# Tiles at multiples of 2048 bytes, and seven pieces of side work moved, in a two-block transformer kernel

## The chip, the cores and the metric

The kernel runs on one core of a Trainium2 chip, as one program. The metric is the time of the whole program on the device, in microseconds (us); less is better. A core has a matrix engine (TensorE, PE in the rows; PEld is its weight load), a vector engine (VectorE, DVE), a scalar engine (ScalarE, ACT), GpSimd (POOL), and SyncE (SP), from which most transfers are issued. Each engine takes its instructions in the order of the program; semaphores hold an instruction back until what it reads is there.

## The reference

Two blocks of a transformer on 256 tokens of width 2048, in float32. The first block has four mixers side by side (sparse attention, a short convolution, a spatial gating unit and stick-breaking attention), an output projection and a gated FFN; the second has an attention layer and a retention layer, each followed by a layer norm.

```
def first_block(x, ...):
    h = rms_norm(x, norm_mix); proj = h @ w_in              # all four mixers' inputs
    o_a = nsa_attention(...); o_b = short_conv_mixer(b_cols, conv_w)
    o_c = spatial_gating_mixer(c_cols, sgu_w, sgu_b); o_d = stick_breaking_attention(...)
    mixed = rms_norm(stack([o_a, o_b, o_c, o_d]), group_gain)
    x = x + mixed @ w_out
    h = rms_norm(x, norm_ffn)
    return x + (silu(h @ w_ffn_gate) * (h @ w_ffn_up)) @ w_ffn_down

def spatial_gating_mixer(cols, sgu_w, sgu_b):
    u, v = split(gelu(cols), 2); v = layer_norm_noaffine(v)
    return u * (tril(sgu_w) applied to v + sgu_b)

def second_block(x, ...):
    x = layer_norm(ALPHA * x + attention_mixer(x, ...), ln_gain[0], ln_bias[0])
    x = layer_norm(ALPHA * x + retention_mixer(x, ...), ln_gain[1], ln_bias[1])
    return x
```

## The kernel before

All weights are streamed once from memory in units of 128 x 1024 values (wf). ScalarE rounds a unit to the F32R format (wh, L375), VectorE takes the rest, wf - wh (wl, L385), and TensorE multiplies with both, so that the product is nearly that of float32. Activations are kept in the same two parts, next to each other in one tile of 512 columns. job_T holds 128 x 128 of the weights and moves an activation tile: for each pair, 512 columns against wh (L452) and 256 against wl (L453). A unit is eight such pairs. job_N holds activations and moves weights (L475 to L477). The stages in the order of time are: the input projection with the four mixers (to about 326 us), the output projection wo (to 435), the FFN (to 1225), attention 2 (to about 1518), retention (to 2280), and the last layer norm and the output (to 2297.5).

Between the weight matmuls the rest of the computation is woven in as side tasks, Python generators. Each pair of matmuls counts 325 ns, and with every 650 ns of it each task's counter falls by one; yield n lets a task wait n such steps. At certain places a task is run to its end at once: S.drain, or when a job asks for an operand tile whose task is not done (XS). The order of the program on each engine is thus fixed when the kernel is built, by these steps.

```
def adv(self, ns):
    self.acc += ns
    while self.acc >= self.period:      # 650
        ...
            t[1] -= 1
            if t[1] <= 0 and t[2] and ...: self.step(t)
```

Side work that the change touches:

- the sparse attention, task A: scores softmax (sm), their transpose (L816), the product with vc (L821);
- the gating unit, task C: gelu of u (cu) and v (cv) by POOL, VectorE and ScalarE (gq), the norm of v (L1043), the product with sg (L1048, called pz in the code), its norm, its transposes (L725) and the scaled operand tiles xB[8] to xB[11] (L732 on ScalarE, L738 on VectorE);
- the convolution, task B: by_task filters slice i and ends with a product on POOL (L1077); ev_bb takes the gate's accumulator of slice i, adds its two halves (ev_sum: ScalarE copies one half, evt, L662; VectorE adds the other, evs, L664), multiplies into braw and accumulates the squares in bacc, on POOL for the slices 0 to 2 and on VectorE for slice 3; then come the column sums (pcs), the reciprocal root, a diagonal matrix bdg (L545), the product pb (L548) that spreads it, and the tiles xB[12] to xB[15];
- wo(0), the first of four output jobs, in eight chunks of one unit each; it reads xB in order, two tiles to a chunk, so chunk 4 starts with xB[8];
- in attention 2, og_task: the gating of head h (L1522) and the split of the result into the operand xA (L509, L511);
- LN.stat: the sums lns (POOL) and sums of squares lnq (L1372) of the first layer norm, and next to it gain, the operand xg of retention (L1648, L1651);
- the end: VectorE finds mean and scale of the 256 rows, nm is -mean times scale; TensorE transposes it (L1993), multiplies it with the gain rows gr and adds the bias (L2004, six products in float32 over two rows), and VectorE finishes six of the eight output tiles with it (L2011); SyncE and ScalarE send them.

## Time and profile before

| | us |
|---|---|
| median of 3 runs | 2287.87 (2285.02 to 2290.71) |
| the profiled execution | 2299.29 |
| its span, first to last instruction | 2297.5 |
| TensorE busy | 2271.2 |
| VectorE busy | 1534.2 |
| ScalarE busy | 1134.2 |
| POOL busy | 406.4 |
| moved by the transfers | 409.82 MB, 178 GB/s over the span |

The profiled execution is a single one, 11.4 us above the median of the unprofiled runs. Busy times are shares of its span; where an engine stands idle only counts if another one has nothing else to do at that moment. The end of the span lies 3.3 us behind VectorE's last operation.

### The profile page before, as it was taken

How to read it: one execution, taken by the hardware profiler on the slowest of the kernel's cores; microseconds unless marked ns; L12 is line 12 of the kernel's file. 1: busy time of each engine (PE TensorE's matmuls, PEld its weight loads, DVE VectorE, ACT ScalarE, POOL GpSimd, SP SyncE). 2: the span in 40 equal slices, each digit the busy share in tenths (PEclk: the TensorE clock that was granted, in tenths of full speed). 3: DMA queues.
4: the chain of work that ended last, by engine and by line, in shares of the span. 5: the costliest groups of instructions: out<-in, count | busy, mean ns of one | idle time of the engine just before them, and what ended most of it. 6: DMA issues, size and time to landing. Idle time of an engine off the chain costs nothing.

```text
span 2297.5 us, 32746 instructions
## 1 busy us (share of the span) xinstructions
PE 2271.2 (99%) x12423; PEld 1946.4 (85%) x12423; DVE 1534.2 (67%) x2368; ACT 1134.2 (49%) x1661; POOL 406.4 (18%) x384
## 2 busy tenths in 40 slices
PE   8999999999999999999999999999999999999998
PEld 7877888888888888888888888898888888888886
DVE  6666697755555565555558898888776676766554
ACT  5457545544443354444444556555444544445442
POOL 2224341111110011110002211742000000001120
PEclk9999999999999999999999999999999999999998
DMA  7643355565565555656565444555555555556553
GB/s 248 231 147 119 111 187 189 184 187 189 187 191 189 179 190 187 188 184 190 186 201 183 141 152 153 179 168 199 175 167 174 183 167 187 168 174 216 189 179 118
DMA packets 113757, 409.82 MB, mean 178 GB/s; under 512 B 12816, under 2 KB 13072, under 8 KB 113342
## 3 DMA queue, kind: packets, MB, share of 16 engines
q1 hardware_dynamic: 111456, 399.75, 54.1%
q0 software_dynamic: 1424, 6.86, 0.9%
q8 instruction: 97, 1.59, 0.3%
q10 hardware_dynamic: 720, 1.13, 0.1%
q14 instruction: 60, 0.49, 0.1%
HBM read 405.57 MB, written 4.21 MB: 178 GB/s over the span
## 4 chain that ended last, share of the span: by engine, by line
PE 87%; DVE 5%; ACT 1%; issue 1%; POOL 1%; POOLq 0%; DVEq 0%; ACTq 0%
PE st L452 39%; PE st L453 20%; PE st L475 7%; PE st L477 7%; PE st L476 7%; DVE wl L385 2%; PE mO L1889 1%; PE mA L855 1%; PE mS L1862 0%; PE st L443 0%; PE st L441 0%; PE st L442 0%; PE st L2004 0%; PE mO L836 0%; PE mT L1907 0%
## 5 line engine op out<-in xcount | busy, mean ns | idle before, releaser
L375 ACT ACTIVATE wh<-wf 128x1024 fp32r<-128x1024 f32 (+1 forms) x750 | 789.7, 1055 | 731.7 <-PE st L452 381.1
L385 DVE TENSOR_TENSOR wl<-wf,wh 128x1024 fp32r<-128x1024 f32 (+1 forms) x750 | 954.8, 1282 | 287.8 <-ACT wh L375 287.1
L452 PE MATMUL st<-xA,wh 128*128 128x512 f32 x2016 | 722.6, 402 | 8.1 <-DVE xA L515 6.8
L453 PE MATMUL st<-xA,wl 128*128 128x256 f32 x2016 | 567.8, 282 | 1.7 <-DVE wl L385 1.5
L452 PE MATMUL st<-xB,wh 128*128 128x512 f32 x1440 | 511.4, 399 | 2.4 <-DVE evs L664 1.8
L452 PEld LDWEIGHTS st<-xA,wh 128*128 128x128 f32 x2016 | 380.9, 189 | 100.9 <-DVE xA L515 6.7
L453 PE MATMUL st<-xB,wl 128*128 128x256 f32 x1440 | 404.3, 281 | 0.0
L453 PEld LDWEIGHTS st<-xA,wl 128*128 128x128 f32 x2016 | 382.6, 190 | 2.9 <-DVE wl L385 2.5
L452 PEld LDWEIGHTS st<-xB,wh 128*128 128x128 f32 x1440 | 271.3, 188 | 67.0 <-DVE evs L664 2.5
L453 PEld LDWEIGHTS st<-xB,wl 128*128 128x128 f32 x1440 | 272.4, 189 | 1.0
L452 PE MATMUL st<-act,wh 128*128 128x512 f32 x704 | 248.8, 399 | 0.0
L453 PE MATMUL st<-act,wl 128*128 128x256 f32 x704 | 197.9, 281 | 0.0
L475 PE MATMUL st<-wh,xB 128*128 128x512 f32 x448 | 175.5, 392 | 0.0
L476 PE MATMUL st<-wl,xB 128*128 128x512 f32 x448 | 174.7, 390 | 0.0
L477 PE MATMUL st<-wh,xB 128*128 128x512 f32 x448 | 174.6, 390 | 0.0
L452 PEld LDWEIGHTS st<-act,wh 128*128 128x128 f32 x704 | 132.4, 188 | 32.9
L664 DVE TENSOR_TENSOR evs<-st,evt 128x256 f32<-128x256 f32 x110 | 46.2, 423 | 145.6 <-ACT evt L662 145.4
L453 PEld LDWEIGHTS st<-act,wl 128*128 128x128 f32 x704 | 133.0, 189 | 0.0
L475 PE MATMUL st<-wh,xA 128*128 128x512 f32 (+2 forms) x320 | 122.6, 383 | 0.0
L476 PE MATMUL st<-wl,xA 128*128 128x512 f32 (+2 forms) x320 | 118.3, 370 | 0.9 <-DVE wl L385 0.9
L477 PE MATMUL st<-wh,xA 128*128 128x512 f32 (+2 forms) x320 | 118.4, 370 | 0.0
L1211 POOL TENSOR_TENSOR evs<-evs,R 128x256 f32<-128x256 f32 x44 | 32.4, 735 | 484.5 <-DVE evs L664 484.5
(447 smaller groups left out, 2611.7 us busy)
## 6 DMA issues: line engine op xcount, KB each, us to landing
wf<-in_w_c SPq DMA_DIRECT2D x264, 512.0 KB, 4.2
wf<-in_w_e SPq DMA_DIRECT2D x256, 512.0 KB, 3.8
wf<-in_w_d SPq DMA_DIRECT2D x112, 512.0 KB, 3.5
wf<-in_w_a SPq DMA_DIRECT2D x84, 512.0 KB, 3.6
wf<-in_w_b SPq DMA_DIRECT2D x32, 512.0 KB, 4.3
xr<-in_xT SPq DMA_DIRECT2D x16, 256.0 KB, 5.4
wf<-in_w_a SPq DMA_DIRECT2D x5, 420.0 KB, 3.8
dr<-d POOLq DMA_DIRECT2D x1, 2048.0 KB, 10.1
```

The source lines that it names most:

```text
L375: ACT.activation(wh[q][:, :n], wf[q][:, :n], AF.Copy)
L385: V.tensor_tensor(wl[q][:, :n], wf[q][:, :n], wh[q][:, :n].bitcast(F32), OP.subtract)
L452: PE.matmul(ps[m], hv[:, cs], x, start=kk == 0, stop=False)
L453: PE.matmul(ps[m][:, :T], lv[:, cs], x[:, :T], start=False, stop=kk == K - 1)
L475: PE.matmul(p, xh, h[:, o:o + n], start=kk == 0, stop=False)
L476: PE.matmul(p, xh, l[:, o:o + n], start=False, stop=False)
L477: PE.matmul(p, xl, h[:, o:o + n], start=False, stop=kk == K - 1)
L664: V.tensor_tensor(s, p[:, :T], t, OP.add)
L855: PE.matmul(pv[:, y, :], qT[i // 2][64 * g:64 * g + 64, i % 2, tt * P:tt * P + P], kT[64 * g:64 * g + 64, b, 0:W], start=True, stop=True)
L1211: G.tensor_tensor(s, s, R2, OP.mult)
L1889: PE.matmul(po, l[:, st_, o], r_[:, st_], start=i == 0, stop=i == 5)
```

## The change

Eight edits. The tile deps and the tile gq8, each of one column, become the two columns of one tile, so that every tile laid out behind them, from wf on, begins 32 bytes lower: the weight and operand tiles go from 32 bytes past a multiple of 2048 to that multiple. In task A two waits go from 1 to 3 and from 1 to 2 steps. In task C the wait ahead of pz goes from 1 to 5. ev_bb(2), the last convolution gate, copies the whole accumulator with ScalarE (evc) and adds the halves on POOL. wo(0) takes its last two chunks tile by tile. og_task of the heads 13 to 15 waits 1 step, not 10. The squares of the first layer norm's tiles 12 to 15 are added on POOL. At the end, gain and bias rows are prepared as five rows in F32R (gain in parts for the three rows of nm in parts, bias in two), so that the six products run in F32R; nm is made of both halves by one operation and split by two more.

```diff
-    deps = pc.tile([P, 1], F32, name="deps")
+    two = pc.tile([P, 2], F32, name="two")
+    deps, gq8 = two[:, 0:1], two[:, 1:2]
...
             V.tensor_tensor(w, w, cmk[:, None, 15 * tt:15 * tt + nk].to_broadcast([P, 8, nk]), OP.mult)
-            yield 1
+            yield 3
             pt = mA()
             PE.transpose(pt[:120, :P], sc, ident)
             pcT = small(128)
             V.tensor_copy(pcT[:120], pt[:120, :P])
-            yield 1
+            yield 2
...
-    gq8 = pc.tile([P, 1], F32, name="gq8")
...
             u = yield from gelu2(cu[tt], 512, s2)
-            yield 1
+            yield 5
             pz = mA()
...
     def ev_bb(i0):
         def f(m, p):
             i = i0 + m
-            s = ev_sum(p)
+            if i0:
+                c = s2("evc")
+                ACT.activation(c, p, AF.Copy)
+                s = c[:, :T]
+                G.tensor_tensor(s, s, c[:, T:], OP.add)
+            else:
+                s = ev_sum(p)
             S.drain(tBy[i])
...
-    job_T(take(), xB, ev_wo(0))
+    job_T(take(), xB, ev_wo(0), 2)
...
-                (G if k < 12 else V).tensor_tensor(self.q, self.q, sq, OP.add)
+                (G if k < 12 or self.done else V).tensor_tensor(self.q, self.q, sq, OP.add)
...
-        yield 10
+        yield 10 if h < 13 else 1
         yield from split(x, s)
...
-    gr = q5.tile([P, D], F32, name="gr")
-    G.dma_start(gr[:2], a["lnv"])
...
+    gr = q5.tile([P, 3 * 512], F32R, name="gr")
+    def gr_task():
+        yield 8
+        for m in range(3):
...
+            for z, (lo, hi) in enumerate(((0, 3), (3, 5))):
+                G.dma_start(t[lo:hi], bass.AP(tensor=v.tensor, offset=v.offset + z * D + 512 * m,
+                                              ap=[[0, hi - lo], [1, 512]]))
+            yield 12
+            o = gr[:5, 512 * m:512 * m + 512]
+            ACT.activation(h, t, AF.Copy)
+            V.tensor_tensor(t, t, h.bitcast(F32), OP.subtract)
+            V.tensor_scalar(t, t, pick[:5, 1:2], None, OP.mult)
+            V.scalar_tensor_tensor(o, h.bitcast(F32), pick[:5, 0:1], t, OP.mult, OP.add)
+            yield 4
...
-    for tt in range(2):
-        V.scalar_tensor_tensor(nm[tt][:, 0:1], mv[:, 2 * tt:2 * tt + 1], -1.0, r[:, tt:tt + 1], OP.mult, OP.mult)
+    V.scalar_tensor_tensor(nm, mv[:, 0::2], -1.0, r, OP.mult, OP.mult)
+    V.tensor_copy(nx[:, :, 0:2], nm[:, :, None].to_broadcast([P, 2, 2]))
+    V.tensor_tensor(nx[:, :, 2], nm, nx[:, :, 0].bitcast(F32), OP.subtract)
...
-        PE.matmul(p, nT[tt][:2, :], gr[:2, 512 * m:512 * m + 512], start=True, stop=True)
+        PE.matmul(p, nT[tt][:5, :], gr[:5, 512 * m:512 * m + 512], start=True, stop=True)
```

How this changes the order on the engines, at three places. First POOL at the end of the convolution: L1077 is the filter's last product of slice 3, evs and evc are the gate's sum for a slice, braw, bq and bacc are slice 2. Before:

```order
L706 TENSOR_TENSOR gq<-gq,cu 128x512
L1077 TENSOR_TENSOR evs<-evs,R_121 128x256
L1095 TENSOR_TENSOR braw<-evs 128x256
L1100 TENSOR_TENSOR bq<-braw 128x256
L1101 TENSOR_TENSOR bacc<-bacc,bq 128x256
```

and now, with line numbers of the changed kernel:

```order
L708 TENSOR_TENSOR gq<-gq,cu 128x512
L1078 TENSOR_TENSOR evs<-evs,R_121 128x256
L1095 TENSOR_TENSOR evc<-evc 128x256
L1102 TENSOR_TENSOR braw<-evc,evs 128x256
L1107 TENSOR_TENSOR bq<-braw 128x256
L1108 TENSOR_TENSOR bacc<-bacc,bq 128x256
L1095 TENSOR_TENSOR evc<-evc 128x256
```

Two additions of evc are new on POOL, one ahead of slice 2's three operations and one, for slice 3, behind them. VectorE at the same place, from the last two operations of the filter of slice 3 (evs<-zp) on; gq, L710 and the two behind it are the gating unit. Before:

```order
L1075 SCALAR_TENSOR_TENSOR evs<-zp,vec,evs 128x256
L385 TENSOR_TENSOR wl<-wf,wh 128x1024
L710 SCALAR_TENSOR_TENSOR gq<-gq,cu 128x512
L664 TENSOR_TENSOR evs<-st,evt 128x256
L1049 TENSOR_TENSOR gq<-mA,vec 128x512
L1051 SCALAR_TENSOR_TENSOR gq<-gq 128x512
L664 TENSOR_TENSOR evs<-st,evt 128x256
L1095 TENSOR_TENSOR braw<-evs 128x256
L1100 TENSOR_TENSOR bq<-braw 128x256
L1101 TENSOR_TENSOR bacc<-bacc,bq 128x256
L385 TENSOR_TENSOR wl<-wf,wh 128x1024
```

and now:

```order
L1076 SCALAR_TENSOR_TENSOR evs<-zp,vec,evs 128x256
L386 TENSOR_TENSOR wl<-wf,wh 128x1024
L1102 TENSOR_TENSOR braw<-evc,evs 128x256
L1107 TENSOR_TENSOR bq<-braw 128x256
L1108 TENSOR_TENSOR bacc<-bacc,bq 128x256
L386 TENSOR_TENSOR wl<-wf,wh 128x1024
L712 SCALAR_TENSOR_TENSOR gq<-gq,cu 128x512
L386 TENSOR_TENSOR wl<-wf,wh 128x1024
L1050 TENSOR_TENSOR gq<-mA,vec 128x512
L1052 SCALAR_TENSOR_TENSOR gq<-gq 128x512
L386 TENSOR_TENSOR wl<-wf,wh 128x1024
```

The two additions L664 are gone, the three operations of slice 3 stand right behind one wl, and the gating unit's L710, L1049 and L1051 (now L712, L1050 and L1052) behind them. Third, VectorE at the end of attention 2, where the residual rows (xr), the squares (lnq) and the operand of retention (xg) are made. Before:

```order
L1434 TENSOR_TENSOR xr<-st,xr 128x256
L1372 TENSOR_TENSOR lnq<-lnq,lnt 128x256
L1432 TENSOR_TENSOR xr<-st,xr 128x256
L1434 TENSOR_TENSOR xr<-st,xr 128x256
L1651 SCALAR_TENSOR_TENSOR xg<-xr,vec,xg 128x256
L1372 TENSOR_TENSOR lnq<-lnq,lnt 128x256 x2
L1651 SCALAR_TENSOR_TENSOR xg<-xr,vec,xg 128x256
L385 TENSOR_TENSOR wl<-wf,wh 128x1024 x2
```

and now:

```order
L1441 TENSOR_TENSOR xr<-st,xr 128x256
L1439 TENSOR_TENSOR xr<-st,xr 128x256
L1441 TENSOR_TENSOR xr<-st,xr 128x256
L1658 SCALAR_TENSOR_TENSOR xg<-xr,vec,xg 128x256 x2
L386 TENSOR_TENSOR wl<-wf,wh 128x1024 x2
```

The additions of squares are gone from VectorE; on POOL each now follows the sum lns of its tile.

## Rows read from the trace of the kernel before

**Rows 1.** The page of the profiled execution: the busy time of the engines (with the share of the span and the count of instructions), and its chain of work that ended last, by engine.

```profile
PE 2271.2 (99%) x12423; PEld 1946.4 (85%) x12423; DVE 1534.2 (67%) x2368; ACT 1134.2 (49%) x1661; POOL 406.4 (18%) x384
PE 87%; DVE 5%; ACT 1%; issue 1%; POOL 1%; POOLq 0%; DVEq 0%; ACTq 0%
```

**Rows 2.** First the view of stretches, TensorE alone, of two stretches in which nothing but the weight matmuls of L452 and L453 runs but for a few: bounds, length, busy time and count of matmuls, granted clock, DMA share, GB/s. Then, from the page, the three groups of the line L452: count, busy time and mean duration of one, and the idle time before them with its releaser.

```profile
365.00:435.00 70.00, 70.00 (x407) 1.00 0.57 187
450.00:520.00 70.00, 70.00 (x398) 1.00 0.63 194
...
L452 PE MATMUL st<-xA,wh 128*128 128x512 f32 x2016 | 722.6, 402 | 8.1 <-DVE xA L515 6.8
L452 PE MATMUL st<-xB,wh 128*128 128x512 f32 x1440 | 511.4, 399 | 2.4 <-DVE evs L664 1.8
L452 PE MATMUL st<-act,wh 128*128 128x512 f32 x704 | 248.8, 399 | 0.0
```

**Rows 3.** The waits of TensorE, by line and by what they waited for: sum in us, number of times, the longest.

```profile
PE mA L816 <- DVE sm L813: 1.2, 2, 0.9
PE mO L821 <- DVE sm L818: 0.4, 1, 0.4
PE mA L1048 <- DVE gq L1043: 1.3, 1, 1.3
PE st L452 <- DVE evs L664: 1.8, 2, 1.1
PE st L452 <- DVE xr L1145: 0.6, 1, 0.6
PE st L452 <- DVE xA L511: 1.3, 2, 0.8
PE st L443 <- DVE wl L385: 1.2, 1, 1.2
PE rt L1993 <- DVE nm L1990: 1.6, 1, 1.6
```

**Rows 4.** Stretches of 10 us from 280 to 340 us (the one from 300 to 310 is left out): bounds, length, busy time and count of PE, PEld, DVE, ACT and POOL, the granted clock, DMA share, GB/s.

```profile
280.00:290.00 10.00, 10.00 (x58) 8.64 (x58) 9.93 (x15) 5.60 (x8) 6.30 (x6) 1.00 0.58 183
290.00:300.00 10.00, 8.70 (x47) 7.53 (x46) 9.51 (x21) 2.57 (x4) 4.58 (x5) 0.83 0.37 108
...
310.00:320.00 10.00, 10.00 (x59) 8.65 (x58) 9.02 (x17) 5.70 (x8) 7.49 (x6) 1.00 0.65 209
320.00:330.00 10.00, 8.16 (x51) 6.87 (x50) 9.55 (x20) 3.95 (x8) 5.55 (x5) 1.00 0.38 130
330.00:340.00 10.00, 10.00 (x52) 8.75 (x52) 8.72 (x28) 3.49 (x9) 0.88 (x1) 0.83 0.57 204
```

**Rows 5.** The timeline of VectorE from 316 to 346 us, and one row of the timeline of TensorE (the last): start, duration, engine, line, operation, tiles, count, and in brackets the idle time before it and its releaser.

```profile
324.96 0.48 DVE L1075 SCALAR_TENSOR_TENSOR evs<-zp,vec,evs 128x256 f32<-128x256 f32 x1
327.64 0.41 DVE L664 TENSOR_TENSOR evs<-st,evt 128x256 f32<-128x256 f32 x1
...
335.27 2.35 DVE L385 TENSOR_TENSOR wl<-wf,wh 128x1024 fp32r<-128x1024 f32 x2
338.06 0.16 DVE L496 TENSOR_SCALAR sm<-pcs 128x2 f32<-128x2 f32 x1 [0.44 <-PE pcs L535]
...
340.22 0.48 DVE L545 TENSOR_SCALAR bdg<-ident,sm 128x128 f32<-128x128 f32 x2
...
341.76 1.12 DVE L738 SCALAR_TENSOR_TENSOR xB<-mA,vec,xB 128x128 fp32r<-128x128 f32 x4
...
342.92 0.40 PE L452 MATMUL st<-xB,wh 128*128 128x512 f32 x1
```

**Rows 6.** The timeline of POOL from 325 to 331 us, the same columns.

```profile
325.52 1.65 POOL L1077 TENSOR_TENSOR evs<-evs,R 128x256 f32<-128x256 f32 x1 [0.88 <-DVE evs L1075]
328.13 0.74 POOL L1095 TENSOR_TENSOR braw<-evs 128x256 f32<-128x256 f32 x1 [0.96 <-DVE evs L664]
328.95 0.94 POOL L1100 TENSOR_TENSOR bq<-braw 128x256 f32<-128x256 f32 x1
329.97 0.91 POOL L1101 TENSOR_TENSOR bacc<-bacc,bq 128x256 f32<-128x256 f32 x1
```

**Rows 7.** The timelines of VectorE, ScalarE and POOL at the end of attention 2, the same columns.

```profile
1519.77 1.50 DVE L1372 TENSOR_TENSOR lnq<-lnq,lnt 128x256 f32<-128x256 f32 x2
1521.18 0.48 DVE L1651 SCALAR_TENSOR_TENSOR xg<-xr,vec,xg 128x256 fp32r<-128x256 f32 x1
1521.58 2.35 DVE L385 TENSOR_TENSOR wl<-wf,wh 128x1024 fp32r<-128x1024 f32 x2
...
1519.87 0.90 ACT L1648 ACTIVATE xg<-xr,vec 128x256 fp32r<-128x256 f32 x2
...
1516.83 0.79 POOL L1370 TENSOR_TENSOR lns<-lns,xr 128x256 f32<-128x256 f32 x1 [0.64 <-DVE xr L1434]
```

**Rows 8.** The timelines of TensorE and VectorE in the last 17 us, the same columns, and of the view of transfers the output on one of its two queues: count, KB each, median us from issue to landing.

```profile
2282.98 10.37 PE L2004 MATMUL st<-gr,nT 2*128 2x512 f32 x12 [0.53 <-ACT nT L1999]
...
2285.46 0.74 DVE L2011 SCALAR_TENSOR_TENSOR y<-y,sm,st 128x512 f32<-128x512 f32 x1
...
2293.45 0.75 DVE L2011 SCALAR_TENSOR_TENSOR y<-y,sm,st 128x512 f32<-128x512 f32 x1 [0.96 <-PE st L2004]
...
out_dram<-y SPq DMA_DIRECT2D x4, 256.0 KB, 2.1
```

More of the change, by code (lines that the diff above doesn't have):

```diff
@@ L267, in pack_inputs @@
     c = shape_consts()
+    out["pick"] = np.ascontiguousarray(np.stack([[1, 0, 1, 1, 0], [0, 1, 0, 0, 1]], 1).astype(np.float32))
     out["lnv"] = np.ascontiguousarray(np.stack([f["ln_gain_2"][1], f["ln_bias_2"][1]]))
@@ L1935, in body @@
     G.dma_start(ob, bass.AP(tensor=v.tensor, offset=v.offset + D + 3 * 512, ap=[[0, P], [1, 512]]))
-    gr = q5.tile([P, D], F32, name="gr")
-    G.dma_start(gr[:2], a["lnv"])
-    nm = [q5.tile([P, 2], F32, name="nm", tag=f"nm{tt}") for tt in range(2)]
-    nT = [q5.tile([P, P], F32, name="nT", tag=f"nT{tt}") for tt in range(2)]
-    for tt in range(2):
-        V.memset(nm[tt][:, 1:2], 1.0)
+    pick = q5.tile([P, 2], F32, name="pick")
+    G.dma_start(pick[:5], a["pick"])
+    gr = q5.tile([P, 3 * 512], F32R, name="gr")
+    def gr_task():
+        yield 8
+        for m in range(3):
+            t = q5.tile([P, 512], F32, name="res", tag="res", bufs=4)[:5]
+            h = q5.tile([P, 512], F32R, name="grh", tag="grh", bufs=1)[:5]
+            for z, (lo, hi) in enumerate(((0, 3), (3, 5))):
[8 more added lines that the diff above has]
+            yield 4
+    S.add(gr_task())
+    nm = q5.tile([P, 2], F32, name="nm")
+    nx = q5.tile([P, 2, 5], F32R, name="nx")
+    nT = [q5.tile([P, P], F32R, name="nT", tag=f"nT{tt}") for tt in range(2)]
+    V.tensor_copy(nx[:, :, 3:5], ones[:, 0:4].rearrange("p (a b) -> p a b", a=2))
     y5 = [q5.tile([P, 4, 512], F32, name="y5", tag=f"y5{tt}") for tt in range(2)]
```

7 lines of the change are left out of this document (3 added, 4 removed).

## The prediction, made before the change was run

> **What bounds the kernel now.** I read the page first. TensorE is busy 2271.2 of 2297.5 us and carries 87% of the chain that ended last [rows 1], so an edit pays only if it shortens what TensorE issues, fills one of its gaps, or cuts the end, where other engines work alone. Next come the stretches. TensorE issues 407 matmuls in one piece of 70 us and 398 in another [rows 2]. The weight products come in pairs, 512 and 256 columns, so a pair takes 70/203.5 = 344 ns here and 70/199 = 352 ns there, at a granted clock of 1.00 (the 2.4 GHz level) in both. 2016 + 1440 + 704 = 4160 such pairs run [rows 2]. Then the waits of TensorE [rows 3]: those which the change aims at come to 1.2 + 0.4 + 1.3 + 1.8 + 0.6 + 1.3 + 1.2 + 1.6 = 9.4 us, none longer than 1.6. The stretches of 10 us show what a wait costs beyond itself: behind the wait of 1.3 at L1048 and behind the two at L452 the granted clock is 0.83 over 10 us, and 52 matmuls issue from 330 to 340 where 58 or 59 do at full clock [rows 4]. Six missing of 58 are 1.0 us and 0.17 of 10 us is 1.7; I take 1.5 us for such a fall to the 1.2 GHz level. Last, the same rows give VectorE 9.93, 9.51, 9.02, 9.55 and 8.72 of 10 us: from 280 to 340 us it is full, which decides what the third and fourth edits are worth.
>
> **The change part by part.** The sum is made against the profiled execution, 2299.29 us (span 2297.5), and carried to the median of the runs shown, 2287.87, as a difference.
>
> *Alignment.* No instruction is added or removed; every tile from wf on moves down 32 bytes. The nearest row is this kernel's own: the tiles act and xB begin at different offsets within 2048 bytes (1312 and 32 bytes, by the order in which the pools lay them out), and L452 takes 399 ns on both [rows 2]. Nothing: 0. The bounds are the two spacings seen, 8 ns apart: 4160 pairs by 8 ns are 33 us if all moved from one to the other. Against the nothing stands a rule of the Trainium skill, "TensorE: Matmul & The Clock Gate", section "Back-to-back issue gap": at the high clock, matmuls without their weight loads start N/2.4 GHz plus about 2.5 ns apart. A pair would take 325 ns by it, and the trace differs by 19 to 27 ns; were all of that an effect of addresses, 4160 pairs would give back some 80 to 110 us, an estimate from that page. Nothing in the trace ties the excess to addresses, so it stays a rival.
>
> *NSA steps (yields 1 to 3 and 1 to 2).* A step is 650 ns of TensorE work, so the transpose at L816 comes 1.3 us later and the product at L821 0.65 more. The longest waits there are 0.9 and 0.4 [rows 3], so both are covered: -1.6 (bounds 0 and -1.6). What is late next is the whole of this task, by some 4 us in all, into the stretch where VectorE is full.
>
> *Gating unit (yield 1 to 5) and the evictions of the last convolution gate.* These go together, because both meet VectorE. Removed: 1.3 us at L1048, 1.8 at L452 [rows 3] and two falls of the clock, 6.1 us if nothing takes their place. VectorE sheds two additions at L664, 0.41 each [rows 5]. But the rows of order show a new wait. VectorE's product braw for the last slice now stands behind only one wl, and reads evc, which POOL adds up last in its queue, after L1077, the first evc, braw, bq and bacc. L1077 starts when VectorE's L1075 ends (324.96 + 0.48 = 325.44). POOL's rows: 1.65 + 0.74 (the new add, by the row of the same form) + 0.74 + 0.94 + 0.91 + 0.74 with six gaps of 0.08 are 6.2 us; all adds at the shortest, 0.74, give 4.9 [rows 6]. VectorE does one wl of 1.2 meanwhile, and so stands still 3.7 to 5.0 us in a stretch in which it had no time over; I take 4.4. Queued behind it are three wl, the gelu and the norm of the gating unit, the norm of the convolution (sm<-pcs) and its bdg; waiting for these are TensorE (wl for each unit of the first output job), its product pb, and the operands xB[8] on. By VectorE's rows [rows 5]: 4.4 less 0.82 for the two L664, less the 0.44 it idled before sm<-pcs, makes bdg 3.1 later, 340.70 + 3.1 = 343.8. Now two wl (2.35) precede L738 instead of one, and its first piece takes a quarter to a third of 1.12: xB[8] is there at about 346.5. TensorE used it at 342.92, 0.8 behind its making. So this place passes 3.6 us later than before, however early TensorE arrives: the removed waits are not gained but spent waiting here, and behind so long a wait the clock falls once more, 1.5. I take +5.0. Bounds: -0.8 (no standstill at all; xB[8] then still comes when it did) and +7 (5.0 of standstill, and up to 1.5 for the NSA work that moves in). The ACT copies of a whole bank end later than the old pair of operations, but TensorE has to wait further on anyway.
>
> *First output job, last two chunks together.* The evictions come twice as far apart; the wait of 0.6 for xr L1145 goes [rows 3]: -0.6 (bound 0).
>
> *Gating of heads 13 to 15 nine steps earlier.* 9 by 0.65 are 5.9 us, so the two waits for xA L511, 1.3 in all [rows 3], mostly go. The last head's ACT copy now stands ahead of a wh, so I leave 0.2: -1.1 (bounds 0 and -1.3).
>
> *Squares of the layer norm on POOL.* VectorE loses the L1372 adds, 1.50 us for two right ahead of wl [rows 7]. The second L1651 can then start when ACT's first of two L1648 ends (1519.87 + 0.45 = 1520.3) and wl 0.4 later, 0.9 earlier than 1521.58. The wait of 1.2 at L443 [rows 3] shrinks to 0.3, and the fall of the clock behind it, half the time by my guess, goes: -1.6 (bounds 0 and -2.7). POOL takes the adds: from 1516.83 it has eight operations of 0.2 to 0.8, done by 1522.5 [rows 7]; TensorE asks for the sums behind L443, later than that.
>
> *The end.* Twelve passes at L2004 take 10.37 us and pace VectorE's six L2011, which start at 2285.46 and, last, 2293.45 with 0.96 idle before it [rows 8]. That is 1.7 us for each of six products. In the F32R form of L452 512 columns are two thirds of a pair, 0.23 us at full clock [rows 2] and 0.46 at half; that makes VectorE the pace: 5 by 0.75 after 2285.46 is 2289.2, 4.2 earlier. One small operation more on VectorE and the five-row copies cost 0.2: -4.0. Bounds -3 (256 KB at 0.75 us apart are 350 GB/s over two queues, and a transfer takes 2.1 us to land [rows 8], so the output may trail) and -4.3. The task that prepares the five rows adds six POOL transfers, three ACT and nine VectorE operations in the last job, where no wait of TensorE is listed [rows 3]: 0, and less than 1 if that cover failed.
>
> Sum: 0 - 1.6 + 5.0 - 0.6 - 1.1 - 1.6 - 4.0 = -3.9. 2299.3 becomes 2295.4 profiled, and 2287.9 - 3.9 = 2284.0 us.
>
> **The rivals.** *No standstill on VectorE* (0.23): POOL's adds run ahead, or the order matters less than I read. Then the third term is -0.8, the sum -9.7, 2278.2 us. For it: POOL is idle 0.88 and 0.96 us between these operations [rows 6]. Against it: each engine takes its queue in order, and five adds can't shrink below 3.7.
>
> *The addresses set the spacing, to the good* (0.09). Most of the 4160 pairs fall to 344 ns: some 3000 by 8 ns are 24, with the rest 2260 us. For it: two spacings exist [rows 2] and nothing in them names a cause. Against it: act and xB alike. The Trainium skill's "DMA: Bandwidth & Descriptors", section "How a descriptor splits into AXI transactions", speaks for a smaller such gain: a start off 256 bytes costs one transaction more. The DMA share of 0.57 to 0.63 [rows 2] says that weights would still not be what is waited for.
>
> *The addresses set the spacing, to the bad* (0.07): slower. 4160 pairs cost 4.2 us for each ns; it decides from 2.6 ns a pair on, (6.9 + 3.9)/4.16; 4 ns give 2287.9 - 3.9 + 16.6 = 2300.6. Against it the same rows.
>
> *The change does little* (0.06): side waits come back one engine further on, and only the end gains, with VectorE's standstill half as long: -4.0 + 2.5 = -1.5, 2286.4.
>
> **How the numbers follow.** The likeliest case (0.55) is the sum, 2284.0. With every bound on one side (a standstill of at least 3.7 us, +2.5, at the low end) it reaches from -8 to +4, 2280 to 2292. 0.3% of this kernel, 6.9 us, is about what a measurement can tell from no change. Faster by more: nearly all of the first and second rival and 0.05 of the main case, 0.35. Slower by more: the third rival and 0.01 of the main case, 0.08. Within: 0.57. The range takes in the first rival with the few us by which runs of one kernel differ (2285.02 to 2290.71), stops just short of the main case's end, where all bounds would have to meet, and leaves out both rivals of addresses: 2271 to 2291.
>
> **What would show it.** Right: VectorE idle about 4 us ahead of braw<-evc with POOL as releaser; a wait of TensorE at pb or at the first product with xB of chunk 4 of the first output job, of 2 us or more in all, and a clock below 1 behind it; no wait left at L816 and L1048; six output steps of VectorE back to back; pairs still 344 to 352 ns. Wrong: no idle VectorE there, or TensorE passing the first output job without a wait (then the first rival); a spacing of pairs outside these two; output transfers that trail the last VectorE step by over 4 us.

## The result, and the profile after

The changed kernel takes 2305.65 us (median of 4 runs, 2303.25 to 2308.17) where the kernel before, run beside it, takes 2286.44 (2284.58 to 2290.71). The ratio is 1.0081 [1.0062, 1.0101]: 19.2 us or 0.8% slower. The forecast was 2284.0 with a range of 2271 to 2291.

The profiled execution took 2306.82 us. Its page answers to [rows 1], the engines' busy time and the chain that ended last:

```profile
PE 2261.7 (98%) x12417; PEld 1949.3 (85%) x12417; DVE 1540.7 (67%) x2371; ACT 1137.2 (49%) x1664; POOL 415.0 (18%) x396
PE 84%; DVE 5%; ACT 1%; POOL 1%; issue 1%; DMA 0%; DVEq 0%; POOLq 0%; ACTq 0%
```

The span is 7.5 us longer than the one shown of before, and TensorE is busy 9.5 us less: it stands still 17 us longer. The waits of TensorE, which answer to [rows 3], say for whom (sum, times, longest):

```profile
PE mA L846 <- POOL pr L873: 8.4, 8, 3.4
...
PE pb L549 <- DVE bdg L546: 2.6, 1, 2.6
PE st L453 <- ACT evc L1093: 2.6, 1, 2.6
PE st L453 <- DVE xB L740: 2.3, 1, 2.3
PE mA L727 <- DVE jk L722: 2.0, 1, 2.0
...
PE mA L857 <- ACT pT L848: 1.4, 2, 0.7
```

Of the waits that the edits aimed at, those at L818 and L823 (L816 and L821 of before), at L1049 and at xr are gone: nothing above 0.1 is left there. The wait in the first chunk of wo(0), for evs before (1.8), is still there, now for evc (2.6). The first line is new in size. L846 transposes the softmax pr of the sparse attention, which the change does not name; in the kernel before the same wait came to 1.3 us in three pieces. The lines pb, evc and xB are those of the gating unit and the last convolution gate; jk is the normed output of the first half of the sparse attention.

The windows of TensorE put these in place (bounds, length, busy time and count of matmuls, granted clock, DMA share, GB/s). First the changed kernel, then the kernel before in a second profiled execution of 2284.11 us (span 2282.3; called the second trace of before from here on):

```profile
100.00:200.00 100.00, 96.36 (x486) 0.98 0.46 149
200.00:300.00 100.00, 91.75 (x474) 0.93 0.30 94
300.00:400.00 100.00, 91.04 (x507) 0.95 0.55 178
500.00:600.00 100.00, 100.00 (x579) 1.00 0.62 190
```

```profile
100.00:200.00 100.00, 97.80 (x499) 1.00 0.46 152
200.00:300.00 100.00, 98.08 (x556) 1.00 0.36 113
300.00:400.00 100.00, 95.63 (x555) 1.00 0.59 198
500.00:600.00 100.00, 100.00 (x579) 1.00 0.61 190
```

From 100 to 400 us TensorE loses 12.4 us of busy time, and of what is left part runs at the lower of the two levels (0.02, 0.07 and 0.05 of 100 us are 14 us of full speed). From 500 to 600 the two kernels issue the same 579 matmuls. The loss lies ahead of the FFN.

To follow it closer, take the time at which TensorE begins each unit of weights, which has the same number in every kernel, and subtract that of the second trace of before. Unit 64 is in the sparse attention, unit 77 follows its end, units 90 to 97 are the eight chunks of wo(0), 94 is its chunk 4, and 122 is the last of the output projection. In us:

| kernel | unit 64 (225.6) | 77 (282.7) | 93 (338.6) | 94 (341.8) | 99 (356.6) | 122 (420.4) |
|---|---|---|---|---|---|---|
| after | 5.6 | 17.4 | 17.1 | 23.9 | 24.4 | 25.6 |
| e1_nsa_back | 0.8 | 0.9 | 0.6 | 7.6 | 8.4 | 9.7 |
| e2_nsa_alone | 6.7 | 15.2 | 16.2 | 16.3 | 16.5 | 16.5 |
| e3_align_alone | 0.9 | 1.0 | 1.0 | 1.0 | 1.0 | 1.0 |
| e4_nsa_gate_back | 1.1 | 1.1 | 1.8 | 6.3 | 7.3 | 8.5 |
| e5_nsa_gate_pz_back | -0.7 | -0.6 | 0.4 | 0.4 | -0.3 | 0.9 |
| e6_nsa_pz_back | -0.3 | -0.2 | 3.5 | 3.5 | 2.9 | 4.1 |
| e9_end_heads_squares | 0.4 | 0.4 | 1.1 | 1.1 | 1.1 | 1.1 |
| e12_nsa_alone_copies_moved | 5.1 | 10.3 | 11.3 | 11.3 | 11.3 | 11.3 |
| e13_nsa_made_up | -3.1 | -1.1 | -0.4 | -0.4 | -0.4 | -0.4 |
| e14_nsa_later_still | -4.6 | 3.0 | 4.8 | 4.8 | 5.0 | 6.2 |

In the changed kernel 17.4 us are lost by unit 77, and 6.8 between units 93 and 94. Behind unit 122 little more happens (25.9 at unit 749) until the end, where the lag falls to 22.7.

**Where the sparse attention stops.** The timeline of ScalarE around 190 us in the kernel before (start, duration, engine, line, operation, tiles, count, and in brackets the idle time before and its releaser):

```profile
189.20 0.51 ACT L867 ACTIVATE pr<-pr,sm 128x256 f32<-128x256 f32 x1 [3.00 <-DVE sm L864]
...
193.97 1.44 ACT L671 ACTIVATE cv<-st,R1c 128x512 f32<-128x512 f32 x2 [0.79 <-PE st L477]
```

The exponential that makes pr runs first; the copies cv of a finished projection come 4.8 us later. The same place in the changed kernel:

```profile
196.98 1.38 ACT L673 ACTIVATE cv<-st,R1c 128x512 f32<-128x512 f32 x2 [4.73 <-PE st L478]
198.38 1.28 ACT L967 ACT_TABLE_LOAD   x1
199.67 0.63 ACT L967 ACTIVATE zm<-zm 128x512 f32<-128x512 f32 x1
200.21 1.04 ACT L376 ACTIVATE wh<-wf 128x1024 fp32r<-128x1024 f32 x1
201.16 0.49 ACT L869 ACTIVATE pr<-pr,sm 128x256 f32<-128x256 f32 x1
...
202.14 0.57 ACT L949 ACTIVATE az<-mB 128x512 f32<-128x512 f32 x1
```

And VectorE, POOL and TensorE of the changed kernel, the same columns:

```profile
195.46 0.69 DVE L866 TENSOR_REDUCE sm<-pr 128x2 f32<-128x512 f32 x1
...
202.75 0.69 DVE L951 TENSOR_SCALAR zm<-mB 128x512 f32<-128x512 f32 x1 [4.63 <-ACT az L949]
203.35 0.68 DVE L952 TENSOR_SCALAR rl<-mB 128x512 f32<-128x512 f32 x1
203.95 0.15 DVE L871 RECIPROCAL sm<-sm 128x2 f32<-128x2 f32 x1
...
204.53 1.80 POOL L873 TENSOR_TENSOR pr<-pr,sm 128x512 f32<-128x512 f32 x1 [3.41 <-ACT wh L376]
...
206.39 0.65 PE L846 MATMUL mA<-ident,pr 128*128 128x128 f32 x4 [3.42 <-POOL pr L873]
```

What the exponential needs, sm, is there at 196.15 (195.46 + 0.69). It runs at 201.16, since the longer waits have moved it behind the cv copies, which stand idle 4.73 us for TensorE's product, and behind a table load, zm and wh. VectorE's reciprocal of its sums then stands behind two operations of the stick-breaking attention, which wait for az, the next on ScalarE. POOL multiplies after it (the profile names wh as its releaser, but VectorE's sm is what came last), and TensorE, which meanwhile had reached L846, stands still 3.42 us. Two queues each put foreign work in front of the same small chain.

This is the longest wait, but not the whole loss. Two more of the waits have the same form. The first stands ahead of it, at the end of the first half of the tokens. VectorE in the kernel before, then VectorE and TensorE in the changed kernel:

```profile
169.34 0.75 DVE L720 TENSOR_SCALAR jk<-mO,sm 128x512 f32<-128x512 f32 x1
170.01 0.95 DVE L956 TENSOR_TENSOR rl<-rl,az 128x512 f32<-128x512 f32 x1
```

```profile
168.19 0.69 DVE L957 TENSOR_TENSOR rl<-rl,az 128x512 f32<-128x512 f32 x1 [3.44 <-ACT az L955]
...
176.06 0.75 DVE L722 TENSOR_SCALAR jk<-mO,sm 128x512 f32<-128x512 f32 x1
...
176.87 0.96 PE L727 MATMUL mA<-ident,jk 128*128 128x128 f32 x4 [2.05 <-DVE jk L722]
```

Before, jk is made ahead of rl, an operation of the stick-breaking attention; now rl stands ahead and waits 3.44 us for ScalarE, and the eleven small operations of the norm ahead of jk take 4.9 us (from 171.04), where they take 2.1 in the second trace of before; TensorE waits 2.05 for jk. The second comes 42 us behind the longest wait, with the other copies of the gating unit, cu (changed kernel):

```profile
240.54 1.32 ACT L673 ACTIVATE cu<-st,R1c 128x512 f32<-128x512 f32 x2 [1.41 <-PE st L478]
...
246.07 0.51 ACT L869 ACTIVATE pr<-pr,sm 128x256 f32<-128x256 f32 x1
...
248.82 1.12 PE L846 MATMUL mA<-ident,pr 128*128 128x128 f32 x4 [1.73 <-POOL pr L873]
```

There the input of the exponential is ready at 241.07 (240.38 + 0.69, VectorE's sm) and it runs 5.0 us later. The lag is 5.6 at unit 64, behind the first two places, and 11.8 more come by unit 77: this third wait, four of 0.5 to 0.8, and most of what the granted clock of 0.93 from 200 to 300 costs.

**Where the gating unit stops.** VectorE, POOL and TensorE from 343 to 366 us in the changed kernel, for [rows 5] and [rows 6]:

```profile
343.45 1.64 POOL L1078 TENSOR_TENSOR evs<-evs,R 128x256 f32<-128x256 f32 x1 [0.36 <-DVE evs L1076]
...
348.06 0.74 POOL L1095 TENSOR_TENSOR evc<-evc 128x256 f32<-128x256 f32 x1
...
348.84 0.43 DVE L1102 TENSOR_TENSOR braw<-evc,evs 128x256 f32<-128x256 f32 x1 [4.33 <-POOL evc L1095]
...
364.71 1.12 DVE L740 SCALAR_TENSOR_TENSOR xB<-mA,vec,xB 128x128 fp32r<-128x128 f32 x4 [1.85 <-ACT xB L734]
...
360.74 0.67 PE L549 MATMUL pb<-bdg,ones 128*128 128x256 f32 x2 [2.59 <-DVE bdg L546]
...
365.11 0.80 PE L453 MATMUL st<-xB,wh 128*128 128x512 f32 x1 [2.29 <-DVE xB L740]
```

VectorE stands still 4.33 us where 4.4 was forecast, POOL's queue is the releaser, and TensorE waits at pb and at the first product of chunk 4, the two places named.

**The end.** TensorE, VectorE and the output transfers of the changed kernel, for [rows 8]:

```profile
2294.94 1.67 PE L2032 MATMUL st<-gr,nT 5*128 5x512 f32 x6 [0.36 <-ACT nT L2027]
...
2297.20 4.03 DVE L2039 SCALAR_TENSOR_TENSOR y<-y,sm,st 128x512 f32<-128x512 f32 x6
...
out_dram<-y SPq DMA_DIRECT2D x4, 256.0 KB, 2.3
```

Six products take 1.67 us, not 10.37, and VectorE's six steps follow each other without a gap, 4.03 us where they took 8.7. From VectorE's first y of the last part (2288.20) to the end of the span are 16.8 us; in the kernel before they are 21.0 (from 2276.49) and, in its second trace, where the twelve passes take 9.33, 20.0 (from 2262.32). So the end is worth 3.2 to 4.2 in the traces.

### The profile page after: what moved, and what is told of

Its sections match the earlier page's. It is cut to its first block, busy times and chain, and to the rows that moved or that the text cites. A ratio compares the mean times of both kernels' runs of the same rounds, so it can differ in the third digit from the quotient of the medians.

```text
span 2305.0 us, 32765 instructions
## 1 busy us (share of the span) xinstructions
PE 2261.7 (98%) x12417; PEld 1949.3 (85%) x12417; DVE 1540.7 (67%) x2371; ACT 1137.2 (49%) x1664; POOL 415.0 (18%) x396
## 4 chain that ended last, share of the span: by engine, by line
PE 84%; DVE 5%; ACT 1%; POOL 1%; issue 1%; DMA 0%; DVEq 0%; POOLq 0%; ACTq 0%
PE st L453 38%; PE st L454 19%; PE st L476 7%; PE st L477 7%; PE st L478 7%; DVE wl L386 2%; PE mO L1896 1%; PE mS L1869 0%; PE st L444 0%; PE st L442 0%; PE mA L857 0%; PE st L443 0%; ACT wh L376 0%; POOL pr L873 0%; PE mT L1914 0%
## 5 line engine op out<-in xcount | busy, mean ns | idle before, releaser
L453 PE MATMUL st<-xA,wh 128*128 128x512 f32 x2016 | 714.3, 397 | 7.3 <-DVE xA L516 6.6
L453 PE MATMUL st<-xB,wh 128*128 128x512 f32 x1440 | 515.8, 401 | 4.9 <-ACT evc L1093 2.6
L453 PEld LDWEIGHTS st<-xA,wh 128*128 128x128 f32 x2016 | 379.8, 188 | 92.5 <-DVE xA L516 6.6
L453 PEld LDWEIGHTS st<-xB,wh 128*128 128x128 f32 x1440 | 272.1, 189 | 71.6 <-ACT evc L1093 2.9
L453 PE MATMUL st<-act,wh 128*128 128x512 f32 x704 | 244.1, 391 | 0.0
L453 PEld LDWEIGHTS st<-act,wh 128*128 128x128 f32 x704 | 131.6, 187 | 28.9
```

What stands on the lines that cost most here:

```text
L453: PE.matmul(ps[m], hv[:, cs], x, start=kk == 0, stop=False)
```

## The experiments

Two theories stand against each other for the 19 us: the lost time comes from the standstill in the gating unit, mis-sized (the forecast's own open term), or from the sparse attention, whose lateness was given no price. Beside them the addresses had to be ruled out.

**e1_nsa_back.** The changed kernel with task A's two waits as before.

```diff
-            yield 3
+            yield 1
             pt = mA()
...
-            yield 2
+            yield 1
             po = pm.tile([P, 512], F32, name="mO", tag="mO", bufs=1)
```

> The changed kernel with the two NSA waits of task A back at 1 and 1; all else as changed. Theory Q (queues): the later steps of task A put its exponential behind ScalarE's copies of the gating unit and behind a table load, so TensorE waits for POOL's pr; that is what costs the first 290 us 17 us. Then this kernel has none of the waits of 3.4, 2.0 and 1.7 us there and takes about 2305.7 - 17 = 2288 us. Theory R (addresses): the tiles at their new places slow the side work of the first stage; then the 17 us stay and it takes about 2305. The pace of the FFN (345 ns a pair in the changed kernel, 352 before) should stay at 345 if the addresses set it.

Measured 2290.28 us (2289.03 to 2291.6), 1.0015 [1.0003, 1.0027] against before: 15.4 us less than the changed kernel. The long waits at L846 fall back to 1.2 in all, and the lag at unit 77 to 0.9. The 8.9 us between units 64 and 122 stay, with VectorE idle 4.32 ahead of braw. So some four fifths of the loss come from two waits of a few steps in task A; the rest is the gating unit's loss, less what the other edits gain.

**e2_nsa_alone.** The kernel before with only these two waits changed (the same lines the other way round).

> The kernel before with the two NSA waits of task A at 3 and 2 and nothing else. Theory Q: +17 us, 2303 us, with the wait for POOL's pr of 3 us or more near 206 us. Theory R: no change, 2286. If the pace of the FFN is set by addresses it stays at 352 ns a pair; if it is set by where TensorE last stood still it may go to 345, and the time is then 13 us less than said.

Measured 2302.03 us (2299.9 to 2316.1), 1.0077 [1.0052, 1.0103]: 16.6 us slower by itself. Its waits of TensorE:

```profile
PE mA L844 <- POOL pr L871: 8.4, 8, 3.4
...
PE mA L725 <- DVE jk L720: 2.0, 1, 2.0
...
PE mA L855 <- ACT pT L846: 1.4, 2, 0.7
```

These are 11.8 us; the kernel before has 1.3 of them, and its 1.2 and 0.4 at L816 and L821 [rows 3] are gone: 8.9 more. Most of the rest is the clock: the granted clock of e2 is 0.98 from 100 to 200 us, 0.95 from 200 to 300 and 0.97 from 300 to 400, where the second trace of before has 1.00 in all three, which is 10 us of full speed. Behind 300 us e2 waits 1.9 less than that trace (1.9 for evs where that has 2.8, and not 1.0 for jk). Together 17.0; the lag at unit 122 is 16.5, and the two profiled executions are 15.8 apart (2299.90 and 2284.11).

**e3_align_alone.** The kernel before with only the shared tile of deps and gq8, so that all tiles behind lie 32 bytes lower.

```diff
-    deps = pc.tile([P, 1], F32, name="deps")
+    two = pc.tile([P, 2], F32, name="two")
+    deps, gq8 = two[:, 0:1], two[:, 1:2]
...
-    gq8 = pc.tile([P, 1], F32, name="gq8")
```

> The kernel before with the one shared tile (every tile from wf on 32 bytes lower) and nothing else. Theory A (addresses set the pace): the pairs of the FFN at 345 ns, 13 to 14 us less, 2273 us. Theory B (the pace is a matter of phase, of where TensorE last stood still): 352 or 345 without rule; the first stage as before in either, 2273 or 2286. Theory R: the first stage 17 us longer, 2303.

Measured 2287.32 us (2284.59 to 2289.58), 1.0002 [0.9989, 1.0015]. The largest group of weight transfers lands in 4.2 us in this kernel and in the kernel before. The addresses are worth nothing that shows (1.9 us by the medians, 0.5 by the ratio, both inside the interval).

**e4_nsa_gate_back.** The changed kernel with task A's waits and the last convolution gate as before, so that of the two edits at the gating unit only the wait of 5 ahead of pz is left.

```diff
-            if i0:
-                c = s2("evc")
-                ACT.activation(c, p, AF.Copy)
-                s = c[:, :T]
-                G.tensor_tensor(s, s, c[:, T:], OP.add)
-            else:
-                s = ev_sum(p)
+            s = ev_sum(p)
```

> The changed kernel with the NSA waits back and the last convolution gate evicted in the old way (ScalarE copies one half, VectorE adds the other). If VectorE's standstill ahead of braw is what costs the first output job 5 to 7 us, this is 5 to 7 us below the kernel that has only the NSA waits back: 2281 to 2283. If the standstill is hidden, no difference between the two. The waits for evc (2.6 us) and for bdg (2.6 us) should be gone or under 1.

Measured 2288.64 us (2286.48 to 2290.43), 1.0008 [0.9999, 1.0018], only 1.6 better than e1: a miss for the theory that the standstill makes the loss. The standstill is gone (the longest idle time of VectorE there is 0.62), but TensorE still waits (for evs 3.8, where the second trace of before has 2.8), and VectorE now waits for pz itself:

```profile
PE st L453 <- DVE evs L666: 3.8, 1, 3.8
...
PE st L453 <- DVE xB L740: 2.3, 1, 2.3
...
PE pb L549 <- DVE bdg L546: 1.2, 1, 1.2
...
336.01 0.69 DVE L1050 TENSOR_TENSOR gq<-mA,vec 128x512 f32<-128x512 f32 x1 [1.57 <-PE mA L1049]
```

A pz four steps later holds chunk 4 up on its own.

**e5_nsa_gate_pz_back** also gives pz its wait of 1 back, and **e6_nsa_pz_back** gives back task A and pz but keeps the new eviction, so that only the standstill is left.

```diff
             u = yield from gelu2(cu[tt], 512, s2)
-            yield 5
+            yield 1
             pz = mA()
```

> The changed kernel with the NSA waits, the eviction of the last convolution gate and the wait ahead of pz all back; what is left of the change is the alignment, the first output job's last two chunks, the heads 13 to 15, the squares on POOL and the end. Theory P (the late product pz and the standstill each hold up chunk 4 of the first output job by themselves): with both gone the 6 us that the kernel with only the gate back still loses there go, and it takes 2282 us or less, some 4 us below the kernel before (the end) plus 1 (the small edits): 2280. Rival S (something else in the changed kernel, the last two chunks together, holds the first output job up): 2288 as with the gate alone back.

> The changed kernel with the NSA waits and the wait ahead of pz back, but the last convolution gate evicted in the new way (whole bank by ScalarE, sum on POOL). Theory P: VectorE's standstill of 4 us ahead of braw remains and by itself holds up bdg, pb and xB[8]: 2285 to 2290, at least 4 us above the kernel with all three back. Rival: only the late pz counts, and this takes 2280 to 2282.

Measured: e5 2282.6 us (2280.27 to 2284.6), 0.9985 [0.9975, 0.9994]; e6 2284.32 (2282.48 to 2286.2), 0.9992 [0.9979, 1.0004]. With e5 near its 2282, the rival that the last two chunks hold the job up falls; e6 stays below the 2285 to 2290 expected of the standstill. In e6 VectorE stands still less long:

```profile
331.21 0.42 DVE L1102 TENSOR_TENSOR braw<-evc,evs 128x256 f32<-128x256 f32 x1 [2.84 <-POOL evc L1095]
```

From these four: late pz alone costs 6.0 (e4 less e5), the standstill alone 1.7 (e6 less e5; 3.2 by the lags at unit 122), both together 7.7 (e1 less e5). By the medians the two add up; by the lags at unit 122, each less e5's 0.9, they do not (7.6 and 3.2, and 8.8 together). They do not act at one place either. e4 loses 4.5 us between units 93 and 94, at chunk 4. e6 loses nothing there but 3.7 between units 77 and 93, in waits of TensorE of 2.05 for VectorE's sm and 2.13 for jk (at 333.75 and 336.26), with a granted clock of 0.72 from 330 to 340. Whether the two delays add up these runs leave open.

**e7_before_again.** The kernel before once more, for a second profile of it; nothing is edited.

> The kernel before, unchanged, once more. If the pace of its FFN (352 ns a pair in the trace of before, 345 in the five other traces) belongs to its addresses or its order, it is 352 again and the execution takes about 2299; if it is a matter of the single execution, 345 and about 2286, as the median of its unprofiled runs says.

Measured 2284.11 us, with the 579 matmuls from 500 to 600 us that were shown above, against 568 in the first profile of before. The same program ran its FFN at both spacings.

**e8_end_alone.** The kernel before with only the new end (the five rows, the task that prepares them, the six products in F32R).

```diff
+    S.add(gr_task())
...
-        PE.matmul(p, nT[tt][:2, :], gr[:2, 512 * m:512 * m + 512], start=True, stop=True)
+        PE.matmul(p, nT[tt][:5, :], gr[:5, 512 * m:512 * m + 512], start=True, stop=True)
```

> The kernel before with the new end alone (the six products in F32R over five rows). The working of the prediction: 4.0 us less, 2281.4 against 2285.4, with VectorE's six last steps 0.72 to 0.75 us apart. Rival: the output transfers trail, or the preparation of the five rows holds up the last job: 2283 to 2286.

Measured 2281.16 us (2279.97 to 2295.94), 0.999 [0.9976, 1.0005]: 4.4 less than before by the medians and near the 2281.4 expected, with an interval that reaches 1. Its six steps of VectorE take 4.03 us, as in the changed kernel.

**e9_end_heads_squares.** The changed kernel without the edits in task A, the gating unit, the convolution gate and wo(0); the alignment, the heads, the squares and the end stay.

```diff
-    job_T(take(), xB, ev_wo(0), 2)
+    job_T(take(), xB, ev_wo(0))
```

> The changed kernel with four edits taken back (NSA waits, last convolution gate, wait ahead of pz, last two chunks of the first output job); left are the new end, the heads 13 to 15, the squares on POOL and the alignment. By the end alone (4.4 us) and by what the traces show at the heads and squares (1.0 and 0.7 us in the kernel with NSA, gate and pz back) it takes 6 us less than before, 2279.5 us, and is faster than both kernels of this change. Rival: the alignment or the small edits cost what they bring, and it stays at 2281 to 2283.

Measured 2282.06 us (2281.17 to 2282.63, 12 runs), 0.9981 [0.9971, 0.999]: faster than both kernels, by 4.2 and 23.6, but in the range of the rival and not at the 2279.5 expected. The end explains all of it. In the lags the six kernels with the edit at the heads gain 0.4 to 1.0 between units 440 and 485 (0.9 here), but the kernels without it also gain up to 0.7 on the second trace of before; by the medians of the two groups the edit is worth 0.4. Of the squares 0.8 show at unit 499, behind the shortened wait at L444 (1.2 before, 0.4 now); by the medians of the same groups 0.7 is left at unit 510 and 0.3 at unit 529.

**e10_nsa_first_half, e11_nsa_second_half.** The kernel before, with the new waits of task A only in the first or only in the second half of the tokens.

```diff
-            yield 1
+            yield 3 if tt == 0 else 1
...
-            yield 1
+            yield 2 if tt == 0 else 1
```

> The kernel before with the longer NSA waits for the first 128 rows only. Both halves of the task run one behind the other, so all steps behind 125 us come 2 us later than before, half of what both give. If the loss grows with the lateness it is 8 us; if it depends on which instruction stands ahead on ScalarE and POOL, it is anything from 0 to 17. Theory Q expects the second: a loss only where the exponential of the scores falls behind a copy that waits for TensorE, seen as a wait for POOL's pr.

> The kernel before with the longer NSA waits for the second 128 rows only (from 184 us on). By lateness alone 8 us or less, all of it behind 184 us, and nothing before; by theory Q again 0 to 17, and the waits at L816 and L821 near 184 us, 0.9 and 0.4, gone.

Measured: 2292.24 us (2289.11 to 2303.34), 1.0027 [1.0013, 1.004], and 2285.47 (2282.53 to 2301.34), 1.0000 [0.998, 1.002]. At unit 122 the first lags by 5.0 and the second leads by 1.0. The sum, about 6, is far from 16.6: the loss is not a price per wait, but of the place at which all of the rest comes to stand. The order on ScalarE shows it. In both kernels the exponential still runs ahead of the cv copies (at 196.57 and 197.58 in e10, 191.48 and 192.48 in e11), and the wait of 3.4 is absent; only with both halves' waits does it fall behind them. In e10 rl stands ahead of jk as in the changed kernel, and TensorE waits 2.05 for jk; in e11 jk is first, and it does not.

**e12_nsa_alone_copies_moved.** e2, with the copies of cv and cu moved from ScalarE to VectorE, so that the exponential cannot stand behind them.

```diff
-            ACT.activation(L[tt][:, :n], p[:, :n], AF.Copy, scale=R1c[:, tt:tt + 1])
+            if nm in ("cv", "cu"):
+                V.tensor_scalar(L[tt][:, :n], p[:, :n], R1c[:, tt:tt + 1], None, OP.mult)
+            else:
+                ACT.activation(L[tt][:, :n], p[:, :n], AF.Copy, scale=R1c[:, tt:tt + 1])
```

> The kernel before with the longer NSA waits, and the four copies of the gating unit's accumulators (cv, cu) made by VectorE instead of ScalarE. Theory Q: in the kernel with the NSA waits alone the exponential stands 5 us behind such a copy, which waits for TensorE; without it pr is ready earlier, the wait of 3.4 us near 206 us goes, and the loss of 16.6 us falls by 3 to 8. Rival: the copy is not what counts (table loads, POOL or VectorE are), and the loss stays at 15 to 18 us.

Measured 2295.68 us (2293.04 to 2308.96), 1.005 [1.0028, 1.0072]: 7.2 less of the loss than e2, within the 3 to 8 expected. Its wait for pr, and ScalarE at the same place:

```profile
PE mA L847 <- POOL pr L874: 5.8, 7, 2.5
...
199.16 0.63 ACT L969 ACTIVATE zm<-zm 128x512 f32<-128x512 f32 x1 [6.07 <-DVE zm L967]
...
200.64 0.50 ACT L870 ACTIVATE pr<-pr,sm 128x256 f32<-128x256 f32 x1
```

The copies no longer stand ahead of the exponential, but zm does, and waits 6.07 us for VectorE, where the cv copies now stand ahead of it. The longest wait at the transpose shrinks only from 3.4 to 2.5. Of the 5.2 us by which e12's lag at unit 122 is below e2's, 1.7 are there by unit 64 and 3.2 more come by unit 77; from 200 to 300 us its granted clock is 0.98 against e2's 0.95. The wait of 1.73 behind the cu copies is gone, the one of 2.05 for jk, where no copy is moved, stays. So the copies are a part of the loss, but what stands next in the queue takes much of their place.

**e13_nsa_made_up, e14_nsa_later_still.** If lateness as such made the loss, taking the lost steps back later in the task should not help where the waits stay, and longer waits should cost more. e13 is e2 with three steps taken out at the end of each half; e14 is the kernel before with waits of 5 and 3.

```diff
-                yield 3
+                yield 3 if n < len(bl) else 2 if n == len(bl) else 1
```

> The kernel before with the longer NSA waits in both halves, and three steps fewer at the end of each half, where only a product is waited for, so that the second half and what follows it run on their old schedule. If what costs 16.6 us is the shift carried into the rest of the task, only a small part is left: 2285 to 2290. If the longer waits themselves cost it, 2300 to 2303.

> The kernel before with the two NSA waits at 5 and 3 steps, 3.9 us later in each half than before against 1.95 with 3 and 2. If the loss grows with the lateness it doubles, to about 2319 us. If it depends on what stands ahead in the queues it is anything else, lower than 2302 too.

Measured: e13 has a median of 2296.86 us (2282.23 to 2298.57), 1.0031 [1.0008, 1.0054], which fits neither expectation, but its ten runs fall into three from 2282.23 to 2283.93 and seven from 2296.14 to 2298.57; the profiled one is of the seven and shows the wide spacing from 500 us on. Ahead of the FFN it leads the kernel before by 0.4, with jk ahead of rl and the exponential ahead of the cv copies as in that kernel. Its wait at the transpose, and that window of TensorE:

```profile
PE mA L844 <- POOL pr L871: 1.6, 3, 1.1
...
500.00:600.00 100.00, 100.00 (x568) 1.00 0.61 185
```

e14 takes 2293.65 us (2289.45 to 2301.34), 1.0047 [1.0028, 1.0065], with 3.7 us of waits at this transpose, the longest 1.8, and a lag of 6.2 at unit 122. Waits of 5 and 3 steps cost 9 us by the medians of few runs (6.2 by the lag), those of 3 and 2 cost 16.6, and those of 3 and 2 with the steps made up cost nothing ahead of the FFN. The loss does not grow with the lateness. In e14 the exponential also stands behind the cv copies, but these find their product ready (at 191.94, without idle time), and it starts at 200.44, when its own input is there (199.72 + 0.69). At jk, rl stands ahead in e14 as well and waits 4.22, but TensorE asks for jk later there and waits 0.50. So to be behind a foreign instruction costs only where that one has to wait itself and TensorE asks for the result before it is through.

## Why the prediction was wrong

It fails at one step, that on task A: "both are covered: -1.6 ... What is late next is the whole of this task, by some 4 us in all, into the stretch where VectorE is full". The first half is right, the two waits at L816 and L821 went. The second half names what is late and gives it no price beyond the upper bound of the gating term ("up to 1.5 for the NSA work that moves in"). Measured it is +16.6 alone, +15.4 in the changed kernel. The forecast followed the two waits that were to be removed, and not the rest of the same task through the queues of ScalarE, VectorE and POOL, where jk now stands behind rl, and pr's exponential behind the copies cv and cu. At the first cv copies the two waits of both halves have put the task 3.9 us later in the order (six steps of 0.65); that took the exponential past copies that wait for TensorE, and it ran 5.0 us after its input was there. For the three waits of 1.7 to 3.4 us the order in the kernels with and without them shows it (at jk the slower norm has a part), and for the copies e12 does, which gives back 7.2 of 16.6. How the rest is shared between jk, the shorter waits and the clock is not separated.

The Trainium skill states the ground for this: "PSUM — Partial Sum Buffer", section "Engine vs sequencer instructions", says that the queues of ScalarE, VectorE and GpSimd strictly keep their order. The trace agrees: the exponential's input is there at 196.15, and it runs at 201.16, behind the copies.

The other steps, in the order of the sum:

| step | forecast | measured | from |
|---|---|---|---|
| alignment | 0 | +0.5 (-2.5 to +3.4) | e3, ratio times 2286 |
| task A | -1.6 | +15.4 | after less e1 |
| gating unit and evictions | +5.0 | +7.7 | e1 less e5 |
| wo(0), last two chunks | -0.6 | +0.5 | e5 less e9 |
| heads 13 to 15 | -1.1 | -0.4 | lag, units 440 to 485, kernels with less without |
| squares | -1.6 | -0.3 | lag, units 498 to 529, kernels with less without |
| the end | -4.0 | -4.4 (3.2 to 4.2 in the traces) | e8 |

They add up to 19.0, of 19.2 measured between the two kernels. Terms that are differences of kernels run at different times are good to an us or so, and the sum with them: the kernel before had medians from 2284.7 to 2286.4 beside them.

*Gating unit.* The mechanism stood as written: 4.33 us of standstill, POOL the releaser, waits at pb (2.59) and at xB of chunk 4 (2.29), the clock below 1 behind them; with that, the rival without a standstill (2278.2) falls. But the term is short by 2.7, and its parts were weighed the wrong way round: the forecast put the loss on the standstill, and e4 to e6 show that the wait of 5 ahead of pz, taken there as a gain that the standstill eats up, costs 6.0 by itself. Nor could all of the 6.1 go that the forecast counted as removed: the wait in the first chunk of wo(0) remained (2.59 for evc at 344.29), and the two falls of the clock that the trace of before shows there, at the same waits, are not in its second trace (1.00 from 280 to 350).

*wo(0).* The wait for xr went, but in the traces of the five kernels with this edit (after, e1, e4, e5 and e6) the units 99 to 122 take 1.2 to 1.3 us longer than in the second trace of before, some 7 ns for each of their 184 pairs. In e2, e3, e9, e12 and e13 it is 0; but e14, which has the edit neither, shows the 1.2 too. The 7 ns are the step between the two spacings described at the end of this text, so it may be no effect of the edit at all; that is open.

*Heads.* One wait of 0.6 for xA is left (1.3 before, 0.8 in the second trace of before), so less went than was taken.

*Squares.* The wait shrank as forecast, from 1.2 to 0.4, and unit 499 comes 0.7 to 0.8 earlier. But the fall of the clock behind it, which was to go, came all the same (0.83 from 1530 to 1540; in the first trace of before 0.83 from 1525 to 1535, in the second none), and 40 us further on more than half of the gain is gone.

*The end.* The mechanism is as forecast, TensorE no longer paces VectorE; the transfers do trail VectorE's last step a little more, by 3.8 us (2305.0 less 2297.20 and 4.03) where 3.3 stood before.

*Alignment.* Both rivals of addresses fall with e3. The sentence of the Trainium skill in "TensorE: Matmul & The Clock Gate", section "Back-to-back issue gap", by which a pair would take 325 ns, has no support in any run here: the pairs stayed at 344 or 352 ns with either layout. Nor did a start on a multiple of 256 bytes, which "DMA: Bandwidth & Descriptors" of the Trainium skill, section "How a descriptor splits into AXI transactions", counts one transaction cheaper, show in the 4.2 us in which the weights land.

*The range.* Without the term of task A the kernel takes 2290.28 (e1), just inside 2271 to 2291, though the gating unit's 7.7 lies above its bound of 7. The bounds of the other named terms were near the mark; the range failed since the largest cost had no bound at all, and no rival named it.

## What to carry over

When a step of a woven task is moved, list every later instruction of the same task on every engine with what now stands ahead of it, and price the longest idle time of that neighbour; the wait that is removed is the smaller part of the matter. A move of 3.9 us made an exponential 5.0 us late where it crossed a copy that waits for TensorE, and a longer move cost less, since the copies there had nothing to wait for. A gain at a wait in the middle of a long run of weight products should be followed for some tens of units, and against more than one trace of the kernel without it, before it is counted to the end.

## What was not expected of the hardware

The same program runs the weight products of a stage at one of two spacings, and which one differs from execution to execution. From 500 to 600 us the first profile of the kernel before issues 568 matmuls and the second 579, which is 352 and 345 ns a pair, both at a granted clock of 1.00. The wide spacing also shows in the profiles of e10, e11 and e13, and the narrow one in all the others; over the FFN it makes 13 to 14 us (the profiles of e10, e11 and e13 lag 13.1 to 13.8 more at unit 485 than at 122). That is why the profiled execution shown before the change was 11.4 us above the median of the runs, and it is the likely reason why e13's runs fall into two groups, of which only one was profiled. One execution can change from one to the other: in units 99 to 122 the changed kernel, e1, e4, e5, e6 and e14 issue a pair some 7 ns wider than the others, and in the FFN they are among the narrow ones; the first trace of before has it the other way round (344 and 352 ns in [rows 2]). What decides it was not found: not the order of the program and not the 32 bytes, since one program does both.
